# Sample keys of the cross-attention: four sequences per tile, turned by VectorE in place

## The chip, the cores and the metric

The kernel runs on one core of a Trainium2 chip. The metric is the device time of one execution in microseconds (us), the median of three runs. A core has a matrix engine (PE), a vector engine (DVE), a scalar engine (ACT), a general engine (POOL) and a queue engine (SP). Matrix products go from the on-chip memory (SBUF, 128 partitions) into accumulators (PSUM, also 128 partitions). Each engine works through its own list in order. Here SP issues the loads of the weights and POOL those of the caches.

## The reference

One layer of a hybrid decoder is computed for a prompt (one sequence of 256 tokens) and, with the same weights, for samples (eight sequences of 4 tokens): two mixing branches with gates, a cross-attention into 256 memory rows, a convolution FFN. What matters here is the cross-attention, in all of fp32:

```
def _cross_attend(hn, mem_k, mem_v, w_cq, w_co):
    Bsz, L, _ = hn.shape
    q = (hn @ w_cq).reshape(Bsz, L, CROSS_HEADS, CROSS_HEAD_DIM).astype(jnp.float32)
    s = jnp.einsum('blhd,bmhd->bhlm', q, mem_k.astype(jnp.float32)) * (CROSS_HEAD_DIM ** -0.5)
    pr = jax.nn.softmax(s, axis=-1)
    o = jnp.einsum('bhlm,bmhd->blhd', pr, mem_v.astype(jnp.float32)).astype(hn.dtype)
    return o.reshape(Bsz, L, D_MODEL) @ w_co
```

There are 4 heads of 512 channels. The samples' keys and values come from caches of shape (8, 256, 4, 512): each sequence has its own 256 memory rows, and one row of one head is 2 KB in a piece. The prompt's keys and values (one sequence) were computed earlier in the kernel and lie in its outputs.

## The kernel before, in words

Activations are held turned, channels on partitions, as 16 tiles of 128 channels by T = 288 tokens: 256 of the prompt, then 32 of the samples (8 sequences times 4). Every product with a weight runs through `proj` (L158) and `proj_w` (L132): a block of 256 output columns, 16 tiles of 128 input channels. SP loads 512 KB of the weight (`raw`, 3 buffers); for each two tiles ACT makes a rounded half `whi` (L103) and DVE the rest `wlo` (L105), each of five buffers, and PE multiplies high by high, high by low and low by high (L147, L148, L151): twelve matmuls for a pair of halves, 96 for a block.

The stages around the change, in order: `gate_b` (L1262) with eight blocks of `w_in`; `w_mix_out` with eight blocks (L1303 to L1309), which reads `x_d` and writes `h_d` by POOL; then the cross-attention. `q_proj(hd)` (L1359) computes a head's queries in two blocks of `w_cq`. The prompt's part is split into halves `qh`, `ql`; the samples' part is put by `diag` (L191) into `xqm`, zeros but for the four columns of each sequence, so that 32 columns can be multiplied with one sequence's keys and only its own rows are not zero. `attend(hd)` (L1380) is the attention of one head. `weave` (L172) runs `q_proj(hd+1)` as the main work and `attend(hd)` as the background, and takes a fixed number of steps of one for each step of the other; for the last head the main work is the beginning of the output projection `w_co`. After this recording a scheduler (L44) may move instructions within each engine's list, except those marked to stay in program order.

`attend` before: POOL loads each sequence's keys of the head as 128 partitions by two rows (`kc`, 512 KB, five buffers `x4`, L1375). PE turns them in eight transposes of 128x128 (`transpose_half`, L1347, L1353) into two PSUM tiles, which DVE and ACT copy to `kT` (L1410, 128x512 each). The scores (L1402) take 4 tiles of 128 channels by 8 sequences, with 32 columns of `xqm` held and 256 memory rows streamed; sequences j and j + 4 add into strip j of 32 partitions of one accumulator `ssc`. So its 128 partitions hold all sequences twice over: four strips, each with the scores of two sequences in their own rows. The prompt's keys are turned in the same way (`kp`, eight transposes), split in halves, and multiplied with `qh` and `ql` (L1431 to L1433). `softmax` (L1338) takes the maximum of a row, the exponential with its sum, the reciprocal, and a multiply on DVE (L1345). The samples' probabilities are turned by two PE transposes (L1446) and copied into `pms` (L1449), again zeros but for each sequence's own columns; the prompt's are turned at L1455. The samples' values (`vq` of the first four sequences in a buffer of its own, `vc` of the others through `x4`) are multiplied with `pms` at L1464 into `osa`, the prompt's at L1474 to L1476. `fold4` (L1484) adds up the four strips.

Of the kernel before, what the change touches and what calls it, by code (L numbers as in the profile page):

```python
# [42 lines left out]
def hybrid_step(ctx: ExitStack, tc: tile.TileContext, I: dict, O: list):  # L43
# [1209 lines left out]
    mx = halves(bigr2, "mx")  # L1253
    pc_cm = pool("pc")
# [48 lines left out]
    for j2 in range(KT // 2):  # L1303
# [4 lines left out]
        if j2 + 3 < KT // 2:  # L1308
            load_x(j2 + 3)  # L1309
    rst.append(acc)  # L1310
# [6 lines left out]
    def x4(name):  # L1317
        return px.tile([P, 2, 512], F32, tag="x4", bufs=5, name=name)

    def k4(name):  # L1320
        return px.tile([P, 4, 256], F32, tag="k4", bufs=5, name=name)

# [3 lines left out]
    def q2(name):  # L1326
        return px.tile([P, 2, 256], F32R, tag="q2", bufs=6, name=name)
# [5 lines left out]
    xqm = [px.tile([P, 4, NB, NS], F32, name=f"xqm{i}") for i in range(2)]  # L1333
# [4 lines left out]
    def softmax(src, n, out):  # L1338
# [6 lines left out]
        V.tensor_scalar(out, out, sm[0:n], None, ALU.mult)  # L1345
# [29 lines left out]
    def mem_rows(src, name):  # L1375
        t = x4(name)
        G.dma_start(out=t, in_=src.rearrange("(m p) d -> p m d", p=P))
        return t

    def attend(hd):  # L1380


        xq = xqm[hd % 2]
        loads = [(I["cache_mem_k"][b, :, hd, :], "kc") for b in range(NB)]
        loads += [(o_pmk[0, :, hd, :], "kp"), (o_pmv[0, :, hd, :], "vp")]
        loads += [(I["cache_mem_v"][b, :, hd, :], "vc") for b in range(4, NB)]
        got = []
        vq = big.tile([P, 4, 2, 512], F32, tag="bigf", bufs=1, name="vq")

        def rows():  # L1390
            while loads and len(got) < 4:
                got.append(mem_rows(*loads.pop(0)))
            return got.pop(0)

        ssc = la_tile()
        kT = []

        def scores(q):
            for d in range(4):
                for j in (3, 2, 1, 0):  # L1400
                    b = 4 * q + j
                    MM(ssc[NS * j:NS * j + NS, 0:256], xq[:, d, b, :], kT[b][:, d, :], start=(q == 0 and d == 0),  # L1402
                       stop=(q == 1 and d == 3))

        for b in range(NB):
            kc = rows()
            kT.append(k4("kT"))
            for d2 in range(2):
                a = transpose_half(kc, d2)
                (S.copy if d2 else V.tensor_copy)(kT[b][:, 2 * d2:2 * d2 + 2, :], a)  # L1410
            if b < 4:
                G.dma_start(out=vq[:, b], in_=I["cache_mem_v"][b, :, hd, :].rearrange("(m p) d -> p m d", p=P))
            yield
            if b == 4:
                scores(0)
                yield
        kp = rows()
        kh, kl = r4("kTh"), r4("kTl")
        for d2 in range(2):
            a = transpose_half(kp, d2)  # L1420
            split(kh[:, 2 * d2:2 * d2 + 2, :], kl[:, 2 * d2:2 * d2 + 2, :], a)
        yield
        scores(1)
        yield
        prs = []
        for l in range(2):
# [7 lines left out]
            if l == 0:  # L1434
                pr = k4("prs")[:, 0, :]
                softmax(ssc[:, 0:256], P, pr)
# [4 lines left out]
        vp = rows()  # L1441
        vh, vl = v2("vph"), v2("vpl")
        split(vh, vl, vp)
        a = mm_tile()
        for m in range(2):
# [294 lines left out]
```

## Time and profile before

| | us |
|---|---|
| runs: median (lowest to highest) | 2558.0 (2557.31 to 2558.45) |
| span of the profiled execution | 2555.0 |
| median less that span | 3.0 |
| busy in the span: PE / DVE / ACT / POOL | 2536.1 / 1733.3 / 1353.1 / 400.0 |
| `gate_b`, then `w_mix_out`, about | 1213 to 1315, then to 1416 |
| cross-attention, first transposed key to last fold | 1443 to 1631 |
| one full head of it | 48.7 |

The span goes from the first to the last instruction of the profiled execution; what lies around it is in the runs' times but not in the trace. Times in the trace count from the start of the span. A matmul in fp32 shows as two records, a PE transpose as one. PE's matmuls overlap, so it is the distance between their starts that adds up, not their lengths. The weight load of a matmul has rows of its own (PEld) and lies beside the matmul before.

### The profile page before, as it was taken

To read this page: it belongs to the slowest core of one execution; us is meant where nothing else is said; L and a number is where in the kernel's file an instruction comes from. 1 tells how busy PE (TensorE), PEld (TensorE's weight loads), DVE (VectorE), ACT (ScalarE), POOL (GpSimd) and SP (SyncE) were. 2 spreads that over 40 slices of the span, in tenths; PEclk is the share of its full clock that TensorE was granted. 3 is DMA by queue.
4 is the path that set the end of the run, shared out by engine and by line. 5 is a ranking of instruction groups with operands and counts; after the bars stand their busy time and mean duration, and the time that the engine had idled before them with its cause. 6 is when DMAs were issued, how large, how long until landed. Compare 5 with 4: busy or idle time off the path is not lost.

```text
span 2555.0 us, 50480 instructions
## 1 busy us (share of the span) xinstructions
PE 2536.1 (99%) x18966; PEld 2440.0 (95%) x18966; DVE 1733.3 (68%) x3672; ACT 1353.1 (53%) x2712; POOL 400.0 (16%) x741
## 2 busy tenths in 40 slices
PE   9999999999999999999999999999999999999998
PEld 8889999999999999999999989999999999999998
DVE  6656777796767666766556555567777677675765
ACT  7656547645364555444545544456545455454545
POOL 3002234241201000010000122412010101020010
PEclk9999999999999999999999999999999999999999
DMA  8676587776868585777666778755555555555553
GB/s 267 216 223 200 170 243 212 225 208 193 233 194 287 171 259 166 242 234 246 184 207 212 250 260 304 221 172 171 166 175 166 175 166 175 167 171 171 169 172 128
DMA packets 442277, 521.96 MB, mean 204 GB/s; under 512 B 27132, under 2 KB 390492, under 8 KB 441968
## 3 DMA queue, kind: packets, MB, share of 16 engines
q1 hardware_dynamic: 407728, 422.34, 53.7%
q0 software_dynamic: 34272, 96.38, 12.2%
q8 instruction: 149, 2.44, 0.4%
q14 instruction: 96, 0.79, 0.1%
q10 hardware_dynamic: 32, 0.01, 0.0%
HBM read 473.13 MB, written 45.48 MB: 203 GB/s over the span
## 4 chain that ended last, share of the span: by engine, by line
PE 96%; DVE 1%; DMA 1%; issue 0%; ACT 0%; POOL 0%; DVEq 0%; ACTq 0%
PE acc L148 27%; PE acc L147 27%; PE acc L151 26%; PE acc L315 2%; PE acc L316 2%; PE acc L319 2%; PE mm L1353 1%; PE la L1402 1%; PE mm L1147 1%; PE la L1138 1%; PE la L1464 1%; PE mm L1111 1%; DMA raw<-in_w_ssd_out_dram 0%; DMA raw<-in_w_in_dram 0%; PE la L864 0%
## 5 line engine op out<-in xcount | busy, mean ns | idle before, releaser
L105 DVE TENSOR_TENSOR wlo<-raw,whi 128x512 fp32r<-128x512 f32 x1464 | 998.4, 687 | 666.3 <-ACT whi L103 636.1
L103 ACT CAST whi<-raw 128x512 fp32r<-128x512 f32 x1464 | 897.9, 618 | 1023.3 <-PE acc L148 807.9
L147 PE MATMUL acc<-xn,whi 128*128 128x288 f32 (+1 forms) x1936 | 550.7, 300 | 0.0
L148 PE MATMUL acc<-xn,whi 128*128 128x288 f32 (+1 forms) x1936 | 542.4, 296 | 0.0
L151 PE MATMUL acc<-xn,wlo 128*128 128x288 f32 (+1 forms) x1936 | 414.5, 295 | 0.0
L148 PE MATMUL acc<-hf,whi 128*128 128x288 f32 x1408 | 393.3, 295 | 0.0
L147 PE MATMUL acc<-hf,whi 128*128 128x288 f32 x1408 | 389.0, 292 | 0.0
L147 PEld LDWEIGHTS acc<-xn,whi 128*128 128x128 f32 (+1 forms) x1936 | 364.9, 188 | 9.8 <-issue 8.1
L148 PEld LDWEIGHTS acc<-xn,whi 128*128 128x128 f32 (+1 forms) x1936 | 365.1, 189 | 6.8 <-issue 4.8
L151 PEld LDWEIGHTS acc<-xn,wlo 128*128 128x128 f32 (+1 forms) x1936 | 310.8, 188 | 1.3 <-issue 1.1
L151 PE MATMUL acc<-hf,wlo 128*128 128x288 f32 x1408 | 294.4, 290 | 0.0
L148 PEld LDWEIGHTS acc<-hf,whi 128*128 128x128 f32 x1408 | 264.5, 188 | 0.1
L147 PEld LDWEIGHTS acc<-hf,whi 128*128 128x128 f32 x1408 | 264.0, 188 | 0.1
L151 PEld LDWEIGHTS acc<-hf,wlo 128*128 128x128 f32 x1408 | 226.3, 188 | 0.0
L148 PE MATMUL acc<-pr,whi 128*128 128x288 f32 x704 | 196.5, 295 | 0.0
L147 PE MATMUL acc<-pr,whi 128*128 128x288 f32 x704 | 195.0, 293 | 0.0
L151 PE MATMUL acc<-pr,wlo 128*128 128x288 f32 x704 | 147.4, 290 | 0.0
L147 PE MATMUL acc<-un,whi 128*128 128x288 f32 x512 | 145.7, 300 | 1.6 <-DVE ma L955 1.6
L148 PE MATMUL acc<-un,whi 128*128 128x288 f32 x512 | 143.0, 294 | 0.0
L1564 POOL COPY fsp<-fst 128x16 f32<-128x16 f32 x88 | 36.3, 415 | 650.2 <-DVE av L1576 426.5
L148 PEld LDWEIGHTS acc<-pr,whi 128*128 128x128 f32 x704 | 132.3, 188 | 0.0
L147 PEld LDWEIGHTS acc<-pr,whi 128*128 128x128 f32 x704 | 132.0, 188 | 0.0
(508 smaller groups left out, 4347.7 us busy)
## 6 DMA issues: line engine op xcount, KB each, us to landing
raw<-in_w_in_dram SPq DMA_DIRECT2D x240, 512.0 KB
raw<-in_w_up_dram SPq DMA_DIRECT2D x176, 512.0 KB
raw<-in_w_down_dram SPq DMA_DIRECT2D x88, 512.0 KB
raw<-in_w_cv_dram SPq DMA_DIRECT2D x32, 512.0 KB
raw<-in_w_ssd_out_dram SPq DMA_DIRECT2D x32, 512.0 KB
sin<-in_state_gla_dram POOLq DMA_DIRECT2D x32, 512.0 KB, 5.9
out_dram<-sin SPq DMA_DIRECT2D x32, 512.0 KB
raw<-in_w_gla_out_dram SPq DMA_DIRECT2D x32, 512.0 KB
```

What stands on the lines that cost most here:

```text
L103: S.copy(hi, raw)
L105: V.tensor_tensor(lo, raw, hi, ALU.subtract)
L147: MM(a, hi[:, k, cs], xh, start=(k0 + s0 + k == 0), stop=False)
L148: MM(a, hi[:, k, cs], xl, start=False, stop=False)
L151: MM(a, lo[:, k, cs], xh, start=False, stop=(k0 + s0 + k == nk - 1))
L315: MM(accs[m], mn_hi[:, kk, ms_], hi[:, 0, :], start=(kk == 0), stop=False)
L316: MM(accs[m], mn_lo[:, kk, ms_], hi[:, 0, :], start=False, stop=False)
L319: MM(accs[m], mn_hi[:, kk, ms_], lo[:, 0, :], start=False, stop=(kk == KT - 1))
L1111: MM(a, kt[:, i, k * P:(k + 1) * P], vt[i], start=True, stop=True)
L1138: MM(osa[NS * j:NS * j + NS, :], qdm[:, k, b, :], sins[b][:, k, :], start=False, stop=(q == 1 and k == 0))
L1147: MM(a, kb[:, k * P:(k + 1) * P], vst, start=True, stop=True)
L1564: G.tensor_copy(sp[:, :, 0:2], st.rearrange("p (b k) -> p b k", k=2))
```

## The change

Keys of the samples. One tile (`ring`, 5 buffers of 1 MB in the pool `pk`) now holds one half of the rows of four sequences: 32 partitions for each sequence, four rows of 2 KB in each partition, loaded by one DMA (`key_load`, four a head: u is which four sequences, th which half of the memory rows). DVE turns blocks of 32x32 in place, 128x512 at a time (`turn32`, four a tile). After that a partition group of 32 holds 32 channels of its own sequence, and a block of 32 columns holds 32 memory rows for each of the four places t. The PE transposes of `kc` and the copies to `kT` are gone. The queries are laid out to match (`spread`): in `xqm`, rows 32s to 32s+31 hold the query channels of sequence s alone, for 16 blocks of 32 channels and two groups of four sequences. The scores take 16 blocks by four (group, half), with 32 columns held and 128 columns streamed, into one strip for each (group, half). A row's 256 scores now lie in two strips, 64 partitions apart, 128 in each.

`softmax_halves` takes the maximum and the sum over both: it copies the partner's column from the other 64 partitions (`swapped`, two copies each time). In both softmaxes the last multiply moves from DVE to ACT. The samples' probabilities need one PE transpose in place of two; memory rows of the values are loaded in pairs to match (`values`).

Loads. The keys of head 0 are loaded in `gate_b`, one tile after every fourth tile of channels, each behind a one-column copy on POOL from `th`; the prompt's rows of head 0 (`rows_load`, keys and values in one tile) and the first four sequences' values (`vq_load`) in the `w_mix_out` stage. In `attend(hd)`: after the scores, the values of the last four sequences (`val_load`, two tiles) and key tiles 0 and 1 of the next head; key tile 2 after the split of the prompt's values; key tile 3, the next head's rows and its `vq` after the value matmuls. All of them are kept in program order on POOL. The keys of head 0 are turned beside `q_proj(0)` in the recording; tiles 0 and 1 of the next head in the last steps of `attend`, tiles 2 and 3 in its first steps. `q2` has 4 buffers in place of 6, and `x4` and `k4` are gone.

```diff
+    pk_cm = pool("pk")
+    pk = pk_cm.__enter__()
+    ktiles = {}
+    def ring(name):
+        return pk.tile([P, 2048], F32, tag="k8", bufs=5, name=name)
+    def key_load(hd, c, after=None):
+        u, th = c // 2, c % 2
+        t = ktiles[hd, "k", c] = ring("kc")
+        if after is not None:
+            G.tensor_copy(t[:, 0:1], after)
+        tc.keep_in_program_order(G.dma_start(
+            out=t.rearrange("p (t d) -> p t d", d=512),
+            in_=I["cache_mem_k"][4 * u:4 * u + 4, :, hd, :].rearrange("s (m t h) d -> h (s m) t d", t=4, h=2)[th]))
...
+    def turn32(t, c):
+        V.transpose(t[:, 512 * c:512 * c + 512], t[:, 512 * c:512 * c + 512])
...
         split_from(*mx(t), th, 0.5)
+        if t % 4 == 3:
+            key_load(0, t // 4, th[:, 0:1])
...
             load_x(j2 + 3)
+        if j2 == 0:
+            rows_load(0)
+        elif j2 < 5:
+            vq_load(0, j2 - 1)
...
-        return px.tile([P, 2, 256], F32R, tag="q2", bufs=6, name=name)
+        return px.tile([P, 2, 256], F32R, tag="q2", bufs=4, name=name)
...
-        V.tensor_scalar(out, out, sm[0:n], None, ALU.mult)
+        S.activation(out, out, ACT.Identity, scale=sm[0:n])
+
+    def swapped(t, name):
+        o = px.tile([P, 1], F32, tag=name, bufs=1, name=name)
+        for e in range(2):
+            V.tensor_copy(o[64 * e:64 * e + 64], t[64 - 64 * e:128 - 64 * e])
+        return o
+
+    def softmax_halves(src, out):
+        mx = px.tile([P, 1], F32, tag="mx", bufs=3, name="mx")
+        V.tensor_reduce(mx, src, axis=AX.X, op=ALU.max)
+        mo = swapped(mx, "mo")
+        V.tensor_scalar(mx, mx, mo, -SC, ALU.max, ALU.mult)
+        sm = px.tile([P, 1], F32, tag="sm", bufs=3, name="sm")
+        S.activation(out.rearrange("p (m t) -> p t m", t=4), src.rearrange("p (t m) -> p t m", t=4), ACT.Exp, scale=SC, bias=mx,
+                     accum_out=sm)
+        so = swapped(sm, "so")
+        V.tensor_tensor(sm, sm, so, ALU.add)
+        V.reciprocal(sm, sm)
+        S.activation(out, out, ACT.Identity, scale=sm)
...
-                qs = px.tile([P, T], F32, tag="qs", bufs=1, name="qs")
-                V.tensor_tensor(qs, a, rc[0], ALU.mult)
-                split(qp[j2][0][:, j, :], qp[j2][1][:, j, :], qs[:, 0:SEQ])
-                diag(xqm[hd % 2][:, d], qs[:, SEQ:T])
+                qs = px.tile([P, SEQ], F32, tag="qs", bufs=1, name="qs")
+                V.tensor_tensor(qs, a[:, 0:SEQ], rc[0][:, 0:SEQ], ALU.mult)
+                split(qp[j2][0][:, j, :], qp[j2][1][:, j, :], qs)
+                V.tensor_tensor(qsm[:, d], a[:, SEQ:T], rc[0][:, SEQ:T], ALU.mult)
...
+    def spread(hd):
+        xq = xqm[hd % 2].rearrange("p (d q) u t -> p q d u t", q=4)
+        for q in range(4):
+            for s_ in range(4):
+                (S.copy if s_ % 2 else V.tensor_copy)(
+                    xq[32 * s_:32 * s_ + 32, q, :, :, 4 * s_:4 * s_ + 4],
+                    qsm[32 * q:32 * q + 32].rearrange("p d (u s l) -> p s d u l", u=2, s=4)[:, s_])
...
-        for b in range(NB):
-            kc = rows()
-            kT.append(k4("kT"))
-            for d2 in range(2):
-                a = transpose_half(kc, d2)
-                (S.copy if d2 else V.tensor_copy)(kT[b][:, 2 * d2:2 * d2 + 2, :], a)
...
+        more = hd < 3
+        spread(hd)
+        yield
+        if hd:
+            for c in (2, 3):
+                for h_ in range(4):
+                    turn32(ktiles[hd, "k", c], h_)
+                    if h_ % 2:
+                        yield
         ssc = la_tile()
+        for j in range(16):
+            for c in (3, 2, 1, 0):
+                u, th = c % 2, c // 2
+                kt = ktiles[hd, "k", 2 * u + th].rearrange("p (t j m) -> p j t m", t=4, j=16)
+                MM(ssc[NS * c:NS * c + NS, 0:P], xq[:, j, u, :], kt[:, j], start=(j == 0), stop=(j == 15))
+        for c in (2, 3):
+            val_load(hd, c)
+        if more:
+            for c in (0, 1):
+                key_load(hd + 1, c)
...
+                pr = px.tile([P, P], F32, tag="prs", bufs=1, name="prs")
+                softmax_halves(ssc[:, 0:P], pr)
...
+        split(vh, vl, kvp[:, 1])
+        if more:
+            key_load(hd + 1, 2)
         a = mm_tile()
+        TR(a[:, 0:P], pr, ident)
...
+        if more:
+            key_load(hd + 1, 3)
+            rows_load(hd + 1)
+            for b in range(4):
+                vq_load(hd + 1, b)
...
             split(*(x[:, 0:SEQ] for x in co(4 * hd + d)), a[:, 0:SEQ])
+            if more:
+                for h_ in range(2):
+                    turn32(ktiles[hd + 1, "k", d // 2], 2 * (d % 2) + h_)
...
-    run(q_proj(0))
+    weave(q_proj(0), first_keys(), 16, 16)
     for hd in range(4):
         main = q_proj(hd + 1) if hd < 3 else chain(steps(wo[0], 6), steps(wo[1], 6))
-        weave(main, attend(hd), 16 if hd < 3 else 12, 21)
+        weave(main, attend(hd), 16 if hd < 3 else 12, 22 if hd else 18)
```

More of the change, by code (lines that the diff above doesn't have):

```diff
@@ L1332, in hybrid_step @@
     SC = 512 ** -0.5
-    xqm = [px.tile([P, 4, NB, NS], F32, name=f"xqm{i}") for i in range(2)]
+    xqm = [px.tile([P, 16, 2, NS], F32, name=f"xqm{i}") for i in range(2)]
+    qsm = px.tile([P, 4, NS], F32, name="qsm")
     pms = px.tile([P, 2, NB, NS], F32, name="pms")
@@ L1380, in attend @@
     def attend(hd):
         xq = xqm[hd % 2]
[L1384 to L1393, printed above, removed]
@@ L1487, in attend, with first_keys @@
         yield
+    def first_keys():
+        for b in range(16):
+            turn32(ktiles[0, "k", b // 4], b % 4)
+            yield
     res = {}
```

64 lines of the change are left out of this document (30 added, 34 removed).

## The prediction, on record before the run

> **What bounds the kernel now.** I read the page first (busy shares, then the chain that ended last), then the busy time by stage, then the chain of waits inside one head of the cross-attention, and then the groups and the DMA of that stage alone.
>
> ```profile
> PE 2536.1 (99%) x18966; PEld 2440.0 (95%) x18966; DVE 1733.3 (68%) x3672; ACT 1353.1 (53%) x2712; POOL 400.0 (16%) x741
> PE 96%; DVE 1%; DMA 1%; issue 0%; ACT 0%; POOL 0%; DVEq 0%; ACTq 0%
> L103 ACT CAST whi<-raw 128x512 fp32r<-128x512 f32 x1464 | 897.9, 618 | 1023.3 <-PE acc L148 807.9
> ```
>
> PE is busy for 99% of the span and makes up 96% of the chain that ended last: a microsecond taken from PE is a microsecond of the kernel, as long as nothing else becomes late. The third line says how late the others are: ACT, which makes the high half of every weight tile, stands idle for 1023 us, 808 of them until PE gives a buffer back. The weight halves are normally made ahead of PE, up to the five buffers of WB.
>
> The change touches the cross-attention. Its heads 1, 2 and 3 by the stage view (columns: window, length, busy us of PE, PEld, DVE, ACT, POOL, clock, DMA share, GB/s):
>
> ```profile
> 1492.30:1541.00 48.70, 48.70 (x425) 43.31 (x423) 27.33 (x59) 21.78 (x45) 12.78 (x18) 1.00 0.85 280
> 1541.00:1589.60 48.60, 48.60 (x424) 43.21 (x423) 27.33 (x59) 21.68 (x45) 12.77 (x18) 1.00 0.84 284
> 1589.60:1631.00 41.40, 40.85 (x365) 35.49 (x364) 21.38 (x43) 18.29 (x36) 10.50 (x17) 1.00 0.76 258
> ```
>
> A full head takes 48.7 us, and PE has no gap in it: it is a pure sum of matmuls at full clock. DVE has 27.3 us of work in that time and the DMA engines are busy for 0.85 of it, so DMA is the next bound, not far away.
>
> **What the change removes on PE.** Chain of waits of head 1 (the shares are of the 48.7 us; pieces are start, length, what):
>
> ```profile
> by line: PE acc L151 18.4%; PE acc L148 17.9%; PE acc L147 17.9%; PE mm L1353 16.4%; PE la L1402 7.9%; PE la L1464 7.3%; PE mm L1432 2.0%; PE mm L1431 2.0%; PE mm L1433 1.9%; PE mm L1474 1.9%; PE mm L1475 1.9%; PE mm L1476 1.9%; PE mm L1484
> 1504.52 1.86 PE la L1402 x32
> 1506.71 0.87 PE mm L1353 x8
> ...
> 1515.21 1.00 PE la L1402 x16
> 1517.33 1.00 PE la L1402 x16
> ```
>
> L1353 is the transpose on PE: 64 of a head's sample keys and 8 of the prompt keys. 16.4% of 48.7 us is 8.0 us for 72, 0.111 each; a block of eight takes 0.87, 0.109 each. I use 0.110. The 64 transposes of sample keys go, the 8 stay: 64 x 0.110 = 7.04 us a head, **28.2 us** in four heads. The transposed probabilities need one PE transpose in place of two: 4 x 0.11 = **0.4 us**.
>
> **The scores.** L1402 is now 32 matmuls a head with 256 columns; each shows as two records, 64 in all, 1.86 + 1.00 + 1.00 = 3.86 us. Afterwards they are 64 matmuls with 128 columns, 128 records: the same number of columns in pieces half as long. Four records run side by side in four strips of 32 columns of the array, and a set of four takes 1.86/8 = 0.232 us. Whether 128 columns take half of that is seen nowhere for four strips; the nearest are matmuls of 128 columns in two strips:
>
> ```profile
> 314.39 0.39 PE L819 MATMUL mm<-m,xdt 128*64 128x128 f32 x4
> 314.61 0.39 PE L821 MATMUL mm<-ea,st 128*64 128x128 f32 x4
> 314.83 0.39 PE L817 MATMUL mm<-m,xdt 128*64 128x128 f32 x4
> ```
>
> Four records start every 0.22 us, a set of two every 0.11: half of 0.232 for half the columns, so the columns set the time in both. Then 32 sets x 0.11 = 3.5 us a head against 3.86. But both rows also agree in something else: 0.22/4 = 0.055 and 0.232/4 = 0.058 us a record, and no row shows records following each other faster for long. If that is the limit, 128 records take 128 x 0.058 = 7.4 us. Bounds: -0.36 x 4 = -1.4 us and +3.6 x 4 = **+14.3 us**. I take 0, near the end by columns, because those rows have the same number of columns a record, and the set of 0.232 us starts its four records together, which a limit on the record rate would not do.
>
> [...] That record spacing could bind at all is the first rival below.
>
> **What it adds on DVE and ACT.** Groups with their shapes (busy us, mean ns):
>
> ```profile
> L1410 DVE COPY kT<-mm 128x512 f32<-128x512 f32 x32 | 22.0, 687 | 11.2 <-PE mm L1353 11.0
> L878 DVE STREAM_TRANSPOSE st<-sqr 128x512 f32<-128x512 f32 x32 | 21.9, 697 | 0.0
> L1345 DVE TENSOR_SCALAR prp<-prp,sm 128x256 f32<-128x256 f32 x8 | 2.8, 350 | 0.0
> L194 DVE COPY xqm<-qs 128x32 f32<-128x32 f32 x16 | 2.8, 178 | 0.5
> L1344 DVE RECIPROCAL sm<-sm 128x1 f32<-128x1 f32 x12 | 1.9, 156 | 1.3 <-ACT prs L1343 0.7 <-ACT prp L1343 0.6
> L1410 ACT COPY kT<-mm 128x512 f32<-128x512 f32 x32 | 18.7, 586 | 29.8 <-PE mm L1353 29.8
> L1343 ACT ACTIVATE prp<-mm,mx 128x256 f32<-128x256 f32 x8 | 3.8, 473 | 5.2 <-DVE mx L1341 5.2
> ```
>
> A head on DVE, from 27.3 us: minus 8 PSUM copies of 0.687 (5.5), 3 multiplies of 0.35 (1.05), 4 block copies of 0.178 (0.7); plus 16 turns of 128x512 at 0.697, as L878's DVE transposes (11.2), 8 `spread` copies at 0.178 (1.4), 4 separate `qsm` products at about 0.18 (0.7), and some six one-column operations of the two-half softmax at 0.156 (0.9). That gives 34.2 us. ACT loses 8 x 0.586 = 4.7 and gains 8 copies and 3 multiplies, about 2.8. With PE at 48.7 - 7.04 - 0.1 = 41.5 us, DVE is busy for 82% of a head and ACT for half: by sums alone PE hides both, and these edits cost 0. The longer softmax of the samples (four copies, one sum, two of them on each side of the exponential) adds about 1 us to a chain under which PE has projection matmuls to run. Head 0's sixteen turns stand, in the instruction order of the changed kernel, in the stage of `gate_b` between weight halves.
>
> **What it adds as waits.** In that order the turns of heads 1 to 3 stand on DVE inside the head before, in front of weight halves (`wlo`), in heads 1 and 2 also in front of the copy into `pms`. DVE works in order: a key tile that lands late holds up the `wlo` behind it, and then PE. So the loads have to be timed:
>
> ```profile
> 1184.00:1326.00 142.00, 142.00 (x1081) 142.00 (x1080) 88.96 (x163) 70.07 (x127) 7.15 (x12) 1.00 0.66 202
> 1486.00:1494.00 8.00, 8.00 (x67) 8.00 (x66) 5.96 (x15) 3.87 (x9) 1.71 (x3) 1.00 1.00 363
> 1494.00:1506.00 12.00, 12.00 (x117) 11.21 (x116) 5.25 (x9) 5.68 (x10) 3.56 (x5) 1.00 1.00 356
> q0 software_dynamic: 774, 2.81, 64.1%
> q1 hardware_dynamic: 1457, 1.44, 35.2%
> q0 software_dynamic: 2569, 9.35, 58.4%
> q1 hardware_dynamic: 4231, 4.20, 25.8%
> DMA to landing us min/median/max: 4.4/6.0/10.3
> 1482.05 2.83 POOL L1377 DMA_DIRECT2D kc<-in_cache_mem_k_dram  x4 [5.78 <-PE la L1464]
> 1440.98 0.29 PE L147 MATMUL acc<-hn,whi 128*128 128x288 f32 x1
> ...
> 1441.78 0.29 PE L147 MATMUL acc<-hn,whi 128*128 128x288 f32 x1
> ```
>
> The first pair of queue lines is of 1494 to 1506 us, the second of head 1 (packets, MB, share). With the engines full they move 356 to 363 GB/s. A head needs 9.35 MB through POOL's queue q0 and 4.20 through SP's: 13.6 MB / 360 GB/s = 38 us, below 41.5 but at 91%. When both queues are loaded q0 gets 2.81 MB / 12 us = 234 GB/s.
>
> After a head's scores POOL issues two value tiles, then key tiles 0 and 1 of the next head (1.05 MB each). Tile 0 is there when 3.15 MB have moved: 8.8 us at 360 GB/s, 13.5 at 234, and some 2 us of issue and landing: 11 to 15.5. What stands before its turn on DVE sums to 9.7 us, about 12 with the softmax's waits. DVE then waits 0 to 3.5 us. Tile 3 is issued only after the value matmuls free a buffer; its 1.05 MB take at least the 4.4 us of half the size, perhaps 7 to 10, and its turn stands 2.8 (tile 2) + 0.7 + 0.85 = 4.4 us behind: a wait of 0 to 5.5 us. The cover: six projection matmuls take 0.80 us, a weight half serves twelve, 1.6 us, and five buffers 8 us when full; in the burst of turns they are rather two or three. I take 2 us of PE stall a head for the three heads in which loads and turns run, **+6 us**, with 0 and 8.5 x 3 = +25 as ends. Head 3 has no turns. Head 0's key loads, 4.2 MB over the eight projections of `gate_b` (8 x 96 matmuls x 0.133 = 102 us), add 41 GB/s to a stage that moves 202 (first stage row), and its turns stand between runs of `wlo`: 0.
>
> **The sum.** -28.2 - 0.4 + 0 + 6 = -22.6 us. The profiled span is 2555.0 and would be 2532.4; the runs' median, 2558.0, lies 3.0 above the span for what is around it, which the change leaves: **2535 us**.
>
> **The rivals.**
> - *Records do not go closer than 0.055 to 0.058 us* (the change does less than it says). Scores take 7.4 us a head: +14.3; PE is then longer under the same DVE work, and the stalls shrink to about 2: 2558 - 28.6 + 14.3 + 2 = 2546. For it: no faster stream of records anywhere. Against it: the column arithmetic above.
> - *No stall at all.* The buffers cover every wait: 2558 - 28.6 - 0 to 1.4 = 2528 to 2529. For it: in heads 1 and 2 PE has no gap today although loads come in the same bursts.
> - *Key tiles late on DVE.* q0 gets 234 GB/s or less whenever DVE needs it: 5 us a head in three heads, 2558 - 28.6 + 15 = 2544; up to 2553.
> - *Slower.* The same place, closed to a loop: the scores free the buffers, tile 0's turn waits for 3.15 MB, `pms` waits behind the turn, the value matmuls for `pms`, tile 3's load for them, its turn for the load, and the next scores for that turn. It gives back all from 28.6/3 = 9.5 us a head. At 253 GB/s, about what the third stage row shows, 13.6 MB take 54 us a head: 3 x 12.5 = +37, 2567. Against it: 356 to 363 GB/s in full stretches, and tile 3's turn has some 14 us before the next scores.
>
> **How the numbers follow.** Chances: forecast (2530 to 2541) 0.52; no stall 0.15; record spacing 0.17; key tiles late 0.10; slower 0.06. About 0.2% is what a measurement here can tell from no change, so faster means under 2552.9 and slower over 2563.1. Faster gets 0.52 + 0.15 + 0.17 + 0.08 = 0.92, the end of the late tiles 0.02 is the same, slower 0.06. The range 2526 to 2549 leaves out the slower case, the upper end of the late tiles and of the record spacing, about 0.12.
>
> **What would show it.** No PE transposes of `kc`; 64 score matmuls a head in 3.5 us (7.4 says the first rival); full heads of 41.5 to 45 us; `wlo` on PE's list of releasers only for a few us; DVE waiting for the key loads at the turns of tiles 0 and 3, under 5 us each; DMA share above 0.9 in heads 0 to 2. Wrong if a head stays above 46 us, or if turns of 128x512 in place take far from 0.70 us.

## The result, and the profile after

| | before | changed | changed / before (95%) |
|---|---|---|---|
| runs, us: median (lowest to highest) | 2557.65 (2553.11 to 2558.45), 4 runs | 2529.2 (2524.11 to 2531.09), 4 runs | 0.9892 (0.9877 to 0.9907) |
| span of the profiled execution, us | 2555.0 | 2529.1 | |

The kernel became 28 us faster. The forecast was 2535, with a range of 2526 to 2549: the time lies in the range, but below the band of the likeliest case (2530 to 2541), close to where the rival "no stall at all" had put it (2528 to 2529).

The page of the changed kernel: the busy shares, the chain that ended last, and the costliest group.

```profile
PE 2508.4 (99%) x18962; PEld 2418.5 (96%) x18962; DVE 1747.9 (69%) x3744; ACT 1342.7 (53%) x2724; POOL 392.2 (16%) x729
PE 96%; DMA 2%; DVE 1%; POOL 1%; ACT 0%; issue 0%; DVEq 0%; ACTq 0%
L103 ACT CAST whi<-raw 128x512 fp32r<-128x512 f32 x1464 | 895.1, 618 | 1016.0 <-PE acc L148 753.2
```

PE lost 27.7 us of busy time and stayed busy for 99%: the kernel is still a sum of matmuls, only a shorter one. ACT still stands idle for 1016 us, most of it until PE gives a buffer back.

The cross-attention by the stage view, with the columns of the prediction (window, length, PE, PEld, DVE, ACT, POOL, clock, DMA share, GB/s); three stretches of about one head each:

```profile
1450.00:1494.00 44.00, 44.00 (x438) 39.83 (x428) 32.15 (x78) 20.56 (x49) 10.05 (x14) 1.00 0.84 300
1494.00:1536.00 42.00, 41.96 (x441) 38.26 (x440) 30.60 (x75) 18.24 (x44) 10.03 (x14) 1.00 0.94 330
1536.00:1576.00 40.00, 39.96 (x405) 36.54 (x409) 32.13 (x79) 20.02 (x49) 10.02 (x14) 1.00 0.92 330
```

PE has no gap worth the name, the clock is full, DVE works 30.6 to 32.2 us of each stretch, and the DMA engines are now busy for 0.92 to 0.94 of two of them.

Runs differ in stages that the change does not touch, so I compare executions by PE itself. The matmuls of the projections (L147, L148, L151) are the same 15984 records in the same order before and after. Cut at the starts that follow the first 6600, 8150 and 9800 of them, each profiled execution falls into four pieces: what lies ahead, then about `gate_b` and `w_mix_out`, then the cross-attention, then the rest up to the end of the span.

| us | first 6600 | to 8150 | to 9800 | to the end |
|---|---|---|---|---|
| before | 1216.92 | 204.08 | 312.65 | 821.32 |
| changed | 1219.15 | 204.08 | 284.54 | 821.31 |
| changed, second execution | 1216.27 | 204.08 | 283.89 | 821.31 |
| changed, third execution | 1212.89 | 204.08 | 285.70 | 821.31 |

The whole change lies in the third piece: 312.65 - 284.54 = 28.1 us less (28.8 and 27.0 in the other two executions). The key loads and turns that moved into `gate_b` cost nothing there: 204.08 in all four. In the first piece, which the change does not touch, the profiled execution of the changed kernel happened to be 2.2 us later; that is why the span fell by 25.9 us only.

The chain of waits of the changed kernel in the second stretch (start, length, what):

```profile
1494.09 3.63 PE la L1468 x128
...
1499.51 0.87 PE mm L1419 x8
```

The 128 score records of a head take 3.63 us, and the only PE transposes of keys that are left are the prompt's eight (L1419).

What the prediction feared was on DVE. Its turns as a group (busy, mean ns, idle before), then two of them in order of time with the wait in front, and PE's whole list of waits in the attention (1445 to 1612):

```profile
L1289 DVE STREAM_TRANSPOSE kc<-kc 128x512 f32<-128x512 f32 x64 | 39.9, 679 | 20.4 <-DMA kc<-in_cache_mem_k_dram 20.4
```
```profile
1510.86 2.49 DVE L1289 STREAM_TRANSPOSE kc<-kc 128x512 f32<-128x512 f32 x4 [1.18 <-DMA kc<-in_cache_mem_k_dram]
...
1528.47 2.49 DVE L1289 STREAM_TRANSPOSE kc<-kc 128x512 f32<-128x512 f32 x4 [3.94 <-DMA kc<-in_cache_mem_k_dram]
```
```profile
PE acc L147 <- ACT co L188: 0.4, 1, 0.4
```

DVE does wait for late keys, 20.4 us in all: 8.2 of them before head 0's turns in `gate_b`, 12.2 in the attention, as the 1.18 us at a tile 0 and the 3.94 us at a tile 3. But that does not reach PE: its list holds one wait of 0.4 us, for something else, and the kernel before has the same one. The stretch around the longest wait says the same:

```profile
1526.00:1533.00 7.00, 7.00 (x57) 7.00 (x56) 4.53 (x11) 1.82 (x6) 0.00 (x0) 1.00 1.02 371
```

The DMA engines are full (1.02 by the records, 371 GB/s), DVE idles 2.5 of 7 us, and PE works through it on weight halves that were made before: from 1523.31 to 1532.29, 9.0 us, DVE finishes no `wlo`, and PE starts 50 projection records in that time, as many as four pairs of halves serve.

### The profile page after: what moved, and what is told of

It reads as the page before. It is cut to its first block, busy times and chain, and to the rows that moved or that the text cites. A ratio compares the mean times of both kernels' runs of the same rounds, so it can differ in the third digit from the quotient of the medians.

```text
span 2529.1 us, 50509 instructions
## 1 busy us (share of the span) xinstructions
PE 2508.4 (99%) x18962; PEld 2418.5 (96%) x18962; DVE 1747.9 (69%) x3744; ACT 1342.7 (53%) x2724; POOL 392.2 (16%) x729
## 4 chain that ended last, share of the span: by engine, by line
PE 96%; DMA 2%; DVE 1%; POOL 1%; ACT 0%; issue 0%; DVEq 0%; ACTq 0%
PE acc L148 27%; PE acc L147 27%; PE acc L151 27%; PE acc L315 2%; PE acc L316 2%; PE acc L319 2%; DMA sqr<-in_state_ssd_dram 1%; PE la L1526 1%; PE la L1468 1%; PE mm L1147 1%; PE la L1138 1%; PE mm L1111 1%; POOL sqr L727 0%; DMA raw<-in_w_gla_out_dram 0%; DMA raw<-in_w_in_dram 0%
## 5 line engine op out<-in xcount | busy, mean ns | idle before, releaser
L147 PE MATMUL acc<-xn,whi 128*128 128x288 f32 (+1 forms) x1936 | 550.5, 299 | 0.0
L148 PE MATMUL acc<-xn,whi 128*128 128x288 f32 (+1 forms) x1936 | 542.3, 296 | 0.0
L151 PE MATMUL acc<-xn,wlo 128*128 128x288 f32 (+1 forms) x1936 | 414.1, 295 | 0.0
L148 PE MATMUL acc<-hf,whi 128*128 128x288 f32 x1408 | 393.2, 295 | 0.0
L147 PE MATMUL acc<-hf,whi 128*128 128x288 f32 x1408 | 389.0, 292 | 0.0
L147 PEld LDWEIGHTS acc<-xn,whi 128*128 128x128 f32 (+1 forms) x1936 | 364.7, 188 | 9.8 <-issue 8.1
L148 PEld LDWEIGHTS acc<-xn,whi 128*128 128x128 f32 (+1 forms) x1936 | 365.0, 189 | 6.8 <-issue 4.9
L151 PEld LDWEIGHTS acc<-xn,wlo 128*128 128x128 f32 (+1 forms) x1936 | 310.5, 188 | 1.3 <-issue 1.1
L151 PE MATMUL acc<-hf,wlo 128*128 128x288 f32 x1408 | 294.5, 290 | 0.0
L148 PEld LDWEIGHTS acc<-hf,whi 128*128 128x128 f32 x1408 | 264.5, 188 | 0.1
L147 PEld LDWEIGHTS acc<-hf,whi 128*128 128x128 f32 x1408 | 264.0, 188 | 0.1
L151 PEld LDWEIGHTS acc<-hf,wlo 128*128 128x128 f32 x1408 | 226.1, 188 | 0.0
L148 PE MATMUL acc<-pr,whi 128*128 128x288 f32 x704 | 196.5, 295 | 0.0
L147 PE MATMUL acc<-pr,whi 128*128 128x288 f32 x704 | 195.0, 293 | 0.0
L147 PE MATMUL acc<-un,whi 128*128 128x288 f32 x512 | 145.8, 300 | 2.2 <-ACT whi L103 1.1
L151 PE MATMUL acc<-pr,wlo 128*128 128x288 f32 x704 | 147.4, 290 | 0.0
L148 PE MATMUL acc<-un,whi 128*128 128x288 f32 x512 | 142.9, 295 | 0.0
L148 PEld LDWEIGHTS acc<-pr,whi 128*128 128x128 f32 x704 | 132.3, 188 | 0.0
L147 PEld LDWEIGHTS acc<-pr,whi 128*128 128x128 f32 x704 | 132.0, 188 | 0.0
```

Of the source, the lines that this page charges most:

```text
L147: MM(a, hi[:, k, cs], xh, start=(k0 + s0 + k == 0), stop=False)
L148: MM(a, hi[:, k, cs], xl, start=False, stop=False)
L151: MM(a, lo[:, k, cs], xh, start=False, stop=(k0 + s0 + k == nk - 1))
```

## The experiments

Theory: PE's sum sets the time, and the buffers of weight halves cover what DVE and the loads do late. The rivals are those of the prediction. Kernels of one group ran on one chip beside the kernel before, whose median there was 2556.06 (first four), 2554.94 (the next four), 2553.58 (the two with three buffers) and 2554.92 (the last two).

**The changed kernel again.** No edit.

> The changed kernel once more, unaltered, so that the kernels beside it on this chip have it to be compared with. Sum-of-PE theory (in the cross-attention PE is never short of anything, so the time is what its matmuls add up to; 256 transposes of 0.110 us less is the gain): 0.989 of the kernel before, about 2529 us. Rival (the gain of the first runs was partly a lucky state of the DMA): 0.991 to 0.994. It also shows whether the one gap of 1.4 us at the weights of w_gla_out, ahead of everything that was changed, comes again.

Measured: 2529.94 us (2527.26 to 2536.13, 5 runs), ratio 0.9904 (0.9890 to 0.9918). That lies between the two forecasts, and the first runs' 0.9892 lies inside its interval. A short stop of PE ahead of the change is there again, 2.2 us at 1200 us.

**Keys before values.** The order of two loads after the scores.

```diff
-        for c in (2, 3):
-            val_load(hd, c)
         if more:
             for c in (0, 1):
                 key_load(hd + 1, c)
+        for c in (2, 3):
+            val_load(hd, c)
```

> Edit: after the scores POOL issues key tiles 0 and 1 of the next head ahead of the two value tiles. Tile 0 then waits for 1.05 MB in place of 3.15, so DVE's waits at tile 0 (0.9, 1.2 and 2.5 us in heads 0 to 2) should go; the value tiles have to be there 15 to 19 us after the scores and need 4.2 MB, 12 to 18 us. Cover theory (weight halves made ahead hide DVE's waits from PE): time within 1 us of the changed kernel. Rival 1 (tile 0's wait reaches PE): 3 to 4 us faster. Rival 2 (values become late): 2 to 4 us slower a head, 6 to 12 us in all.

Measured: 2531.59 us (2527.36 to 2537.75, 5 runs), ratio 0.9907 (0.9891 to 0.9922), not to be told from the unaltered kernel. DVE's waits at tile 0 became shorter, 1.54, 0.51 and 0.66 us in place of 0.90, 1.18 and 2.53, without a gain in time. Its profiled execution (2534.1) shows what a stop costs when there is one. PE's waits in the attention, then the stage view around them:

```profile
PE mm L1514 <- ACT prp L1390: 1.9, 1, 1.9
PE mm L1541 <- DVE co L189: 1.9, 1, 1.9
```
```profile
1528.00:1532.00 4.00, 2.10 (x18) 1.86 (x16) 4.00 (x9) 0.70 (x2) 0.00 (x0) 1.00 0.95 362
1532.00:1536.00 4.00, 4.00 (x46) 3.62 (x49) 2.54 (x6) 1.18 (x3) 0.00 (x0) 0.57 0.79 263
1559.00:1563.00 4.00, 2.08 (x16) 1.75 (x15) 0.69 (x1) 1.49 (x3) 0.00 (x0) 1.00 0.93 328
1563.00:1567.00 4.00, 4.00 (x26) 1.09 (x28) 3.92 (x9) 1.45 (x4) 0.12 (x1) 0.57 0.43 141
```

Each stop of 1.9 us is followed by a stretch with a granted clock of 0.57 in the mean of 4 us: half clock for 3.4 us, so by my estimate 1.7 us lost once more. The third piece of this execution took 291.93 us, 7.4 more than the changed kernel's 284.54: about two times 1.9 + 1.7. The two stops have different sources. Ahead of the first, DVE stands for 3.19 us in front of the turns of a tile 3, which lands just before they begin, and these turns stand in front of the subtraction `co`. Ahead of the second, ACT waits for a late weight tile of `w_co`, with the prompt's softmax behind it.

**The first turns held in place**, between their projection blocks, where the scheduler would move them.

```diff
-            turn32(ktiles[0, "k", b // 4], b % 4)
+            tc.keep_in_program_order(turn32(ktiles[0, "k", b // 4], b % 4))
```

> Edit: the sixteen turns of head 0 stay in program order, beside q_proj(0), where the scheduler had put them into the gate_b stage, and DVE waits for the four loads there (1.9, 2.3, 1.0 and 3.0 us) should go. DVE gets 10.7 us more work in the 34 us before the first scores, where it had 21. Cover theory: 0 to 1 us either way, since PE lost nothing at those waits. Rival (DVE is the nearly full engine and its waits count): 2 to 5 us faster if the waits counted, or 2 to 5 slower if q_proj(0) has no room for the turns.

Measured: 2528.55 us (2524.26 to 2536.70, 5 runs), ratio 0.9899 (0.9884 to 0.9915): the same. DVE's four waits for head 0's keys are gone, and the time stays: where head 0's turns stand makes no difference that can be measured.

**The last multiply of both softmaxes back on DVE.**

```diff
-        S.activation(out, out, ACT.Identity, scale=sm[0:n])
+        V.tensor_scalar(out, out, sm[0:n], None, ALU.mult)
...
-        S.activation(out, out, ACT.Identity, scale=sm)
+        V.tensor_scalar(out, out, sm, None, ALU.mult)
```

> Edit: the last multiply of both softmaxes goes back from ACT to DVE (three a head, about 1 us a head). This undoes one part of the change by itself. Sum-of-PE theory: within 1 us of the changed kernel. Rival (DVE at 32 of 42 us a head is near enough to the bound that what it is spared counts): 1 us a head, 3 to 4 us slower.

Measured: 2531.6 us (2530.02 to 2538.96, 5 runs), ratio 0.9914 (0.9899 to 0.9929): 1.7 us above the unaltered kernel by medians, with intervals that overlap. Its profiled execution (2537.49) holds two instances of what the prediction feared, a late key tile that reaches PE. Two turns on DVE and PE behind the second, in order of time; then PE's list of waits; then the stage view in steps of 2 us, first behind the first instance and then at the second:

```profile
1529.66 2.49 DVE L1289 STREAM_TRANSPOSE kc<-kc 128x512 f32<-128x512 f32 x4 [5.12 <-DMA kc<-in_cache_mem_k_dram]
...
1573.14 2.49 DVE L1289 STREAM_TRANSPOSE kc<-kc 128x512 f32<-128x512 f32 x4 [5.05 <-DMA kc<-in_cache_mem_k_dram]
...
1577.02 0.39 PE L1541 MATMUL mm<-pTh,vph 128*128 128x256 f32 x1 [2.43 <-DVE co L189]
```
```profile
PE mm L1541 <- DVE co L189: 4.5, 2, 2.4
```
```profile
1535.00:1537.00 2.00, 2.00 (x23) 1.83 (x26) 1.90 (x6) 2.00 (x6) 0.00 (x0) 1.00 0.82 298
...
1574.00:1576.00 2.00, 0.59 (x5) 0.35 (x3) 2.00 (x6) 0.02 (x1) 0.00 (x0) 1.00 1.03 418
1576.00:1578.00 2.00, 0.98 (x6) 0.98 (x7) 1.96 (x8) 1.87 (x8) 0.00 (x0) 0.84 1.03 409
1578.00:1580.00 2.00, 2.00 (x14) 1.94 (x17) 1.85 (x8) 1.96 (x6) 0.00 (x0) 0.50 0.77 274
```

At the second, a key tile lands late, DVE stands for 5.05 us in front of its turn, the small subtraction `co` behind it is late, and PE stops for 2.43 us; then PE runs at half clock for 6.8 us. At the first, the wait of 5.12 us leads in the same way to a stop of 2.08 us, and the clock stays full. The third piece is 6.6 us longer than the changed kernel's (291.15). So the chain exists, but through `co`, which PE's L1541 needs done, and not through `wlo`. In the unaltered kernel's three profiled executions (longest waits 3.94, 2.91 and 3.56 us) it did not reach PE. The length of the wait alone does not decide: with keys before values 3.19 us were enough, in another order.

**64 PE transposes a head put back**, of a constant and unread, between the scores and the loads behind them (the weave takes eight more steps to hold them); everything else as changed.

```diff
+        for b in range(8):
+            for d2 in range(2):
+                a = mm_tile()
+                for d in range(4):
+                    TR(a[:, d * P:(d + 1) * P], ident, ident)
+            yield
         for c in (2, 3):
             val_load(hd, c)
...
-        weave(main, attend(hd), 16 if hd < 3 else 12, 22 if hd else 18)
+        weave(main, attend(hd), 16 if hd < 3 else 12, 30 if hd else 26)
```

> Edit: the changed kernel with 64 PE transposes of the unit matrix a head put back, four to a PSUM tile, that nobody reads; no copies, no loads. They do what the removed transposes did to PE and nothing else. Sum-of-PE theory: 256 x 0.109 = 28 us slower than the changed kernel, 1.000 of the kernel before, give or take 2 us. Rival (the gain came from the PSUM copies that ACT and DVE no longer make, or from loads that start earlier): at most 8 us slower.

Measured: 2558.14 us (2553.13 to 2560.32, 10 runs), ratio 1.0011 (1.0002 to 1.0020). The whole gain is gone: about 28 us above the 2529.9 of the changed kernel, or by ratios 1.0011 - 0.9904 = 0.0107 of 2555, 27 us. The third piece takes 314.09 us, 29.5 more than 284.54, for 256 x 0.110 = 28.2. The stage view shows how:

```profile
1450.00:1500.00 50.00, 50.00 (x546) 46.84 (x540) 33.30 (x79) 21.51 (x49) 10.02 (x14) 1.00 0.76 267
1500.00:1549.00 49.00, 49.00 (x437) 45.47 (x430) 30.72 (x74) 18.92 (x42) 10.01 (x14) 1.00 0.81 286
1549.00:1596.00 47.00, 46.92 (x470) 43.03 (x467) 32.90 (x79) 21.43 (x52) 10.00 (x14) 1.00 0.76 273
```

The same DVE work, the same loads, PE as full as ever, and the stretches 6 to 7 us longer. The transposes on PE are what the change removed from the time; nothing hid them.

**Scores of 64 columns**, twice as many matmuls for the same products.

```diff
-                MM(ssc[NS * c:NS * c + NS, 0:P], xq[:, j, u, :], kt[:, j], start=(j == 0), stop=(j == 15))
...
+            for e in range(2):
+                for c in (3, 2, 1, 0):
...
+                    MM(ssc[NS * c:NS * c + NS, 64 * e:64 * e + 64], xq[:, j, u, :], kt[:, j, 2 * e:2 * e + 2],
+                       start=(j == 0 and e == 0), stop=(j == 15 and e == 1))
```

> Edit: each score matmul of 128 columns is cut into two of 64, so 256 records a head in place of 128 with the same columns. Column theory (a set of four strips takes the time of its columns): 64 sets of 0.057 us, 3.6 us a head, no change. Record theory (records do not come faster than the 0.028 us of the changed kernel): 256 x 0.028 = 7.3 us a head, 14.5 us slower in all. In between, the spacing of the records gives the limit itself.

Measured: 2538.02 us (2530.99 to 2540.03, 4 runs), ratio 0.9926 (0.9905 to 0.9948): by ratios 6 us slower than the unaltered kernel, though the two intervals just overlap, and by the third piece (296.61) 12.1 us. It is not for the reason that the rival gave. PE in order of time at head 0's scores:

```profile
1445.61 2.99 PE L1473 MATMUL la<-kc,xqm 128*32 128x64 f32 x197
1450.53 1.08 PE L1473 MATMUL la<-kc,xqm 128*32 128x64 f32 x59 [1.94 <-issue]
```

197 records in 2.99 us less the length of the last: 14 ns apart, half of the changed kernel's 3.63/128 = 28 ns, for half the columns. So neither 55 nor 28 ns is a limit of records; in these, columns set the time. But after 197 records PE stops for 1.94 us, in which it waits for nothing that the profile shows. Between 1447 and 1451 us the queue of instructions brings one load of 16 KB. Heads 1 and 2 have such a stop too, 2.60 us soon behind the scores and 1.70 us in them; head 3 has none of this kind. That PE waited there for its own instructions is my guess; it rests on the moment alone, and no run shows it.

**Every turn of heads 1 to 3 made three times**, and then **those of tile 2 alone** (a block turned three times is turned). The cut is of the second; the first has `range(3)` there and at the turns in the last steps of `attend`.

```diff
-                    turn32(ktiles[hd, "k", c], h_)
+                    for _ in range(3 if c == 2 else 1):
+                        turn32(ktiles[hd, "k", c], h_)
```

> Edit: every turn of heads 1 to 3 is made three times (twice back and forth leaves it as once). DVE gets 32 x 0.67 = 21.4 us more in each of heads 0 to 2, 32 + 21 = 53.5 us against PE's 41.5. If the sums of the engines decide, these heads take 53.5 us: 36 us slower than the changed kernel, 1.003 of the kernel before. If the turns are off the path altogether: 0. If DVE's order, and not its sum, had been the limit: more than 36.

> Edit: only tile 2 of heads 1 to 3 is turned three times, 8 x 0.67 = 5.4 us more DVE work in each of heads 0 to 2, 37.5 against PE's 41.5. Cover theory: 0 to 3 us slower in all, because DVE still fits. Rival (DVE is already the bound in these heads): 5.4 x 3 = 16 us slower.

Measured: all tiles 2579.55 us (2574.01 to 2583.49, 4 runs), ratio 1.0095 (1.0076 to 1.0113); tile 2 alone 2532.33 us (2529.59 to 2537.14, 4 runs), ratio 0.9913 (0.9897 to 0.9930). The stage views, first of tile 2 alone and then of all:

```profile
1449.00:1496.00 47.00, 47.00 (x460) 42.81 (x460) 38.20 (x90) 21.80 (x52) 10.02 (x14) 1.00 0.84 300
1496.00:1540.00 44.00, 44.00 (x447) 40.83 (x446) 36.27 (x85) 19.86 (x47) 10.01 (x14) 1.00 0.85 312
1540.00:1586.00 46.00, 44.08 (x445) 40.79 (x444) 38.10 (x90) 21.44 (x50) 9.98 (x14) 1.00 0.85 308
```
```profile
1449.00:1514.00 65.00, 61.36 (x556) 56.33 (x554) 57.27 (x123) 27.34 (x61) 10.02 (x14) 0.97 0.68 242
1514.00:1577.00 63.00, 55.31 (x487) 51.78 (x486) 55.17 (x120) 22.60 (x54) 10.48 (x15) 0.89 0.67 237
1577.00:1640.00 63.00, 45.92 (x497) 40.79 (x495) 48.82 (x104) 17.69 (x43) 10.93 (x17) 0.81 0.59 215
...
1620.00:1630.00 10.00, 6.17 (x27) 5.78 (x26) 10.00 (x18) 1.69 (x3) 0.00 (x0) 0.50 0.01 2
```

Eight more turns a head (5.4 us of DVE) cost some 2 us for three heads together, by ratios (0.9913 against 0.9904), less than the intervals tell apart; 32 more (22 us) cost 49. So there is a point between them at which DVE begins to set the time; these two runs do not say where. Past it the time is worse than the sum of DVE: the mean stretch took 63.7 us, in which DVE worked 53.8. DVE stood idle for 30 of the 191 us, 16.6 of them until ACT delivered a `whi`, so the order takes part and not the sum alone, as the third theory of the edit has it. The last row shows one thing more: PE, busy for 6.17 of its 10 us, was granted a clock of 0.50 through all of them. DVE is busy throughout that row, so what the half clock adds to the time is not shown.

**Three buffers of weight halves in place of five**, before and after.

```diff
-WB = 5
+WB = 3
```

> Edit: the same in the kernel before, to be the other end of that distance. Fewer buffers cost it what they cost outside of the cross-attention, the same as the changed kernel (0 to 10 us by either theory); in the cross-attention DVE has 27 of 49 us of work and no key loads to wait for, so it should lose at most 2 us there.

> Edit: three buffers in place of five for each kind of weight half, in the changed kernel, everywhere. It takes away 3.2 us of the 8 us by which the halves can be made ahead of PE. Cover theory: DVE's waits for key tiles (0.9 to 3.9 us) then reach PE: the three heads lose 1 to 4 us each, and the distance to the kernel before with three buffers falls from 28 to 16 to 25 us. Rival (there is slack in the order itself, not in the buffers): the distance stays 26 to 30 us.

Measured: before 2593.57 us (2592.96 to 2595.57, 4 runs), ratio 1.0154 (1.0139 to 1.0169); changed 2572.28 us (2568.77 to 2575.12, 4 runs), ratio 1.0065 (1.0048 to 1.0082). The distance falls from 28 to 21.3 us. Both lose 40 us or more, most of it far from the attention, where 0 to 10 us had been expected: the third piece of before takes 314.47 us with three buffers (312.65 with five), that of the changed kernel 290.73 (284.54). There the changed one loses 6.2 us and before 1.8. PE's one long wait in its attention, the chain of waits and ACT ahead of it, and the stage view:

```profile
PE mm L1514 <- ACT prp L1390: 3.3, 1, 3.3
```
```profile
1571.96 13.02 DMA raw<-in_w_cq_dram
```
```profile
1585.07 0.62 ACT L103 CAST whi<-raw 128x512 fp32r<-128x512 f32 x1 [4.56 <-DMA raw<-in_w_cq_dram]
```
```profile
1580.00:1586.00 6.00, 2.88 (x22) 2.65 (x20) 4.36 (x11) 1.44 (x3) 0.00 (x0) 1.00 1.04 411
1586.00:1592.00 6.00, 5.84 (x36) 1.70 (x36) 5.87 (x10) 1.20 (x3) 1.64 (x3) 0.72 0.46 144
```

A weight tile takes 13 us to come beside the bursts of keys and values, ACT stands in front of its `whi`, the prompt's softmax (`prp`) behind that is late, PE stands for half of 6 us, and half clock follows. So with fewer buffers the gain shrinks, inside the 16 to 25 us of the cover theory, but not by the way it gave: DVE's waits for key tiles (up to 3.00 us) do not reach PE here either. That five buffers are what kept the predicted stall small is therefore argued, from the 9.0 us without a new `wlo` above; this run does not show it.

**Values of the first four sequences loaded once**, by head 0; heads 1 to 3 use them again, so their result is another. And the changed kernel a third time, as its pair.

```diff
     def vq_load(hd, b):
+        if hd:
+            vqs[hd] = vqs[0]
+            return
```

> Heads 1 to 3 use the values of the first four sequences that head 0 loaded, so that 2.1 MB of a head's 13.6 MB through the DMA queues are left out (and the output of these heads is another). The question is whether the short stalls in the heads, and with them the runs of the changed kernel above 2531 us, come from key tiles and weights that land late under the full DMA engines. Theory, late loads: the share of the DMA engines falls from 0.92 to 0.94 to about 0.8 in heads 1 and 2, DVE's wait at the turns of tile 3 falls from 2 to 4 us to under 2, no PE stop over 0.5 us is left in the heads, no window at half clock in them, the median goes 1 to 2 us below the unaltered changed kernel, to about 2528, and no run lies above 2533. Rival, the stops and the spread come from elsewhere (other stages, the softmax chain): median within 1 us of the unaltered kernel and runs up to 2536 as before.

> The changed kernel without an edit, as the pair of the run with fewer value loads. Both theories: median 2528 to 2531, single runs from 2524 to 2536, DMA share 0.92 to 0.94 in heads 1 and 2.

Measured: values once 2527.77 us (2522.66 to 2529.47, 4 runs), ratio 0.9895 (0.9878 to 0.9911); the changed kernel 2524.68 us (2522.72 to 2525.76, 4 runs), ratio 0.9880 (0.9865 to 0.9894), below the 2528 to 2531 expected of it. The middle stretch and the wait for keys with values loaded once:

```profile
1494.00:1536.00 42.00, 42.00 (x430) 38.84 (x429) 32.78 (x79) 19.85 (x48) 7.38 (x11) 1.00 0.80 278
```
```profile
DVE kc L1289 <- DMA kc<-in_cache_mem_k_dram: 11.1, 5, 2.8
```

The same wait in the changed kernel, of its pair's execution:

```profile
DVE kc L1289 <- DMA kc<-in_cache_mem_k_dram: 10.2, 6, 3.6
```

The DMA share went from 0.94 to 0.80 as meant, yet DVE waits as long in sum (11.1 us against 10.2), and the time does not fall: the median is 3.1 us higher, with intervals that overlap, and the third pieces are 284.69 and 285.70. So these runs give nothing to the theory that late loads cost the unaltered kernel a measurable part. Nor did the spread become smaller with fewer loads: 6.8 us, against 3.0 of the pair. What else could make the spread stands in the last section.

## Why the prediction was right, and where its size was off

- **The transposes, -28.2.** Right, in the mechanism and in the size. They are gone from the profile, and putting them back took the gain away (27 to 29.5 us).
- **One transpose of probabilities, -0.4.** Too small to be seen alone.
- **The scores, taken as 0.** The chain says 3.63 us a head against 3.86: -0.9 in four heads, within the bounds of -1.4 and +14.3 and near the end by columns. The rival "records do not go closer than 0.055 us" is refuted twice, by 28 ns in the change and by 14 ns at 64 columns. The four records of a set start 7 ns apart; the next set follows 109 ns later in the changed kernel (128 columns), 216 ns in the kernel before (256 columns).
- **Work on DVE and ACT, 0.** Right. DVE was to work 34.2 us a head and works 94.9/3 = 31.6 (the three stretches), 2.6 less; a turn takes 679 ns against the 697 assumed. A small one, in busy us and mean ns:

```profile
L1447 DVE COPY xqm<-qsm 32x32 f32<-32x32 f32 x32 | 5.5, 172 | 0.6
```

  The assumed 178 and 156 were close: 172, and 148 for the one-column copies of the two-half softmax. The multiplies moved to ACT could have stayed, and head 0's turns could stand elsewhere, without a difference that these runs can tell.
- **The waits on DVE.** Right in place and size: at tile 0 they were 0.90, 1.18 and 2.53 us (forecast 0 to 3.5), at tile 3 2.31, 3.94 and 1.37 (0 to 5.5).
- **The stall of PE, +6. This step failed**, in the sentence "a key tile that lands late holds up the `wlo` behind it, and then PE". PE's list of waits has 0.4 us in place of the 6, and the kernel before has those too. By records the third piece fell by 28.1 us; the terms on PE give 28.2 + 0.4 + 0.9 = 29.5, which leaves 1.4 us for stops and for all errors of the terms, 0.7 and 2.6 in the two other executions. I had set the cover at "rather two or three" buffers in the burst of turns. At the wait of 3.94 us the halves already made lasted for 9.0 us, with four pairs of them used. The way was wrong as well: where a late key tile did reach PE (multiply on DVE, keys before values) it came through `co`, at PE's L1541, with stops of 1.9 to 2.4 us, and not through `wlo`. With three buffers 4 (by the third piece) to 7 (by the runs) of the 28 us go, but there by a late weight tile.
- **The sum.** Span 2532.4 forecast, 2529.1 measured: -4.6 for the stall (with the errors of the terms), -0.9 for the scores, +2.2 for a later start of the stages around the change, lost ahead of them. That later start is luck: it brought the forecast nearer. The run of that profile took 2530.86, 1.8 above its span, where I had put 3.0 around it. In every run with both on record the two differ by 1.7 to 1.9, so the 3.0 held some 1.2 us of difference between two executions. The third measurement of the changed kernel, 2524.68, lies under the lower end of the range.
- **DMA.** 0.94 and 0.92 in heads 1 and 2, as forecast above 0.9; in the first stretch 0.84, where I had said the same. The queue's load of a stretch:

```profile
q0 software_dynamic: 2519, 9.41, 62.0%
q1 hardware_dynamic: 4420, 4.40, 31.5%
kc<-in_cache_mem_k_dram POOLq DMA_DIRECT2D x4, 1024.0 KB, 9.6
```

  9.41 + 4.40 = 13.8 MB (forecast 13.6), and the four key tiles of that stretch land after 9.6 us in the median. Tile 3 took 9.6, 9.3 and 7.0 us in the three heads, inside the "7 to 10"; tile 0 took 10.8, 10.0 and 11.4, at or under the low end of "11 to 15.5". The "some 2 us of issue and landing" in that estimate stand in no row of the prediction; the nearest in the profile before is `mg_d<-mq`, 288 KB that landed 2.6 us after their issue in the median, 1.8 more than they take at 360 GB/s.
- **The slower rival**, the loop through tile 3, did not close: with 0.92 to 0.94 the loads still fit. Turned three times, the keys did make the heads longer than the sum of DVE.

## What to carry to other kernels

When PE makes up the whole chain, count what leaves PE by the distance of its starts and trust it; moving the work to an engine with a quarter of its time free (DVE, busy for 94.9 of 126 us with the new work) was worth nearly the whole sum here, 28.1 of 29.5 us. Before pricing a stall, set the wait against the buffers between the late engine and PE, and then look for everything else that stands behind the late operation: a wait of 3.94 us in front of five buffers of weight halves cost nothing, and where waits of 3.2 to 5.1 us did reach PE, it was by a small subtraction that no such buffer covers. And compare executions by the same records on the bounding engine, piece by piece; single runs of one kernel beside each other differed by up to 12 us here, and part of that lies far from the edit.

## What the runs showed of the hardware

**A short stop can cost twice.** After stops of PE of 1.9 and 1.9 us (keys before values), 2.4 (the multiply on DVE) and 3.3 (three buffers) the granted clock fell to half: 0.50 in the rows of the multiply on DVE, for 6.8 us in all; 0.57 and 0.72 as means of 4 and 6 us in the others, 3.4 us each if the level was 0.50 there too. Not every stop does it. The 2.08 us at 1531 us with the multiply on DVE left the clock at 1.00; its mean from 1447 to 1610 us is 0.98, which the 6.8 us behind the other stop account for. And behind the 1.94 us in head 0's scores of 64 columns the records went on as closely as before, the next 59 in 1.08 us. So 1.9 us without matmuls was enough to draw half clock in one place, and 2.08 us drew none in another. What decides between such stops is open.

**The same matmuls, three spacings.** The projections of `gate_b` and `w_mix_out` stand in the same order on PE in the changed kernel and its variants. The rows below are of one stretch of the stage view, of the changed kernel, the one with the multiply on DVE and the one with values loaded once, in that order; the number to read is the count behind PE.

```profile
1250.00:1280.00 30.00, 30.00 (x230) 30.00 (x230) 18.68 (x35) 14.50 (x27) 1.49 (x3) 1.00 0.81 251
```
```profile
1250.00:1280.00 30.00, 30.00 (x226) 30.00 (x225) 20.95 (x39) 15.02 (x29) 1.49 (x3) 1.00 0.67 210
```
```profile
1250.00:1280.00 30.00, 30.00 (x233) 30.00 (x233) 22.55 (x44) 15.54 (x31) 1.49 (x3) 1.00 0.75 224
```

230, 226 and 233 in 30 us at full clock, and over the 1550 records of the two stages a mean spacing of 131.7, 134.4 and 130.4 ns: their piece takes 204.08, 208.39 or 202.06 us. Five of the variants' profiled executions have the 208.39, both kernels of the comparison 204.08 (with three buffers it is 206.26 and 208.24). What sets it is open. Together with the first piece (1212.89 to 1219.15 us in three executions of the changed kernel) it is as large as the spread of the runs, about 12 us, and would account for that without the loads; that it does is argued, since only the profiled executions show their pieces. The first piece goes by one stop far from the change for a good part: at about 572 us PE waits at L890 for ACT (`cst`), 1.6, 2.4 and 5.5 us in the executions with 1212.89, 1216.27 and 1219.15, and only the last has 6.8 us of half clock around it.
